# Gathering selected key and value blocks as pairs in rows of eight tokens, in a hybrid attention and convolution layer

## The chip, the cores and the metric

The kernel runs on one core of a Trainium2 chip as one program. The metric is device time in microseconds (us) of one execution; before the change it is 1492.12 us, the median of 3 runs (1490.02 to 1495.15). Engines are named as in the profile: PE is TensorE, PEld its weight loads, DVE VectorE, ACT ScalarE, POOL GpSimd, SP the engine that only issues transfers.

## The reference

One inference step of one decoder layer, for a prompt of 1024 tokens and for 8 samples of 4 new tokens each with 8192 past tokens in paged caches. One projection of the normalised input gives queries, three key/value sets, gates and the input of a convolution module. What the change touches is one of three attention branches of the samples: per query and group of heads, the 16 best of 128 blocks of 64 tokens are attended to. Three blocks (the first, the last cached one, the new one) are always among them. Cut to what matters:

```
forced = (j == 0) | (j == cur) | (j == cur - 1)
score = jnp.where(forced[None, :, None, :], FORCED_SCORE, imp)
_, idx = lax.top_k(score, n_top)                       # n_top = 16
k_sel = ks_bg[b_i, g_i, idx].reshape(B, N_KV, Q, n_sel, HEAD_DIM)
v_sel = vs_bg[b_i, g_i, idx].reshape(B, N_KV, Q, n_sel, HEAD_DIM)
s_s = jnp.einsum('bqghd,bgqnd->bqghn', qf, k_sel)
p_s = masked_softmax(s_s, m_s)
o_s = jnp.einsum('bqghn,bgqnd->bqghd', p_s.astype(v_sel.dtype), v_sel)
```

So per query and group there are 13 chosen blocks and 2 forced cached ones, besides the 4 new tokens.

## The kernel before, in words

The program has three phases that share one projection of weight tiles (`project`, lines 241 to 255: three matmuls of 352 columns for each piece, lines 183 to 185). Phase 1 (to about 565 us) normalises the input, gathers all compressed-branch pages (`load_pool`, line 503) and ends with `choose` (line 716), which ranks the blocks and writes `idxs`, a table of row numbers for the gathers. Phase 2 (about 565 to 920 us) interleaves three streams by `_weave` (line 1194): `sample_stream` (the selected blocks and the window branch), `conv_ins` (projections, named mm in the rows), and `conv_stream` (31 convolution taps on DVE, line 1157). Phase 3 is the prompt's attention and the output projections.

In phase 2 there are 8 units u. A unit is one group of heads g and two samples times four new tokens. The cached tables are seen as rows of four tokens (2 KB, line 137), so a block of 64 tokens is 16 rows, and one gather (`gather`, line 933) of 128 rows fills a tile of 128 partitions x 512 with one chosen block for each of 8 (sample, token) pairs.

- `slc_keys(u)` (line 947) loops over 7 steps of two tiles each: 13 gathers into `KG` (6 buffers, `KB`) and, as the fourteenth, a tile of forced blocks. ACT copies the group's half of each tile to `kg` (line 975), PE turns it (two transposes, line 978), ACT copies the four turned pieces to `skT` (line 982), PE multiplies with the queries (line 956), and DVE adds a mask while it writes the scores (line 959).
- `slc_vals(u)` (line 1022) runs beside the keys of unit u+1: four steps, each with four gathers into `VG` (6 buffers, `VB`; the last step has one), transposes of the scores (line 1044), a copy (line 1052), and the products of the step before (line 1034).
- `forced` (line 939) gathers the forced blocks of four samples at once into `Fk_slc` and `Fv_slc`: four gathers in all, with row numbers `idxF` made at the start of phase 1 (lines 369 to 382, with DVE's line 378).

Each engine works its instructions in order. The order is set when the program is built, by a scheduler that runs a timeline of its own. The gathers all stand in POOL's queue, KG and VG mixed; each waits there until its buffer is free, and those behind it wait too. A buffer of KG is free when ACT's copy has read it, one of VG when PE's products have.

## Time and profile before

| | |
|---|---|
| median of 3 runs | 1492.12 us |
| the profiled execution | 1496.63 us, span 1494.8 us |
| PE busy | 1370.8 us (92%) |
| DVE, ACT, POOL busy | 1094.9 us (73%), 729.5 us (49%), 786.2 us (53%) |
| mean granted TensorE clock | 0.969 of full |
| gathers KG, VG | 104 and 104, busy 123.3 and 113.5 us on POOL |
| moved by software queue q0 (all gathers) | 122.71 MB in 37440 packets |

Busy time is the time in which an engine had an instruction of its own running. The idle time before a group of instructions is named with what ended it. Matmuls are pipelined, so the durations of single ones overlap. The granted clock is a share of full speed in the stretch that the row names.

### The profile page before, as it was taken

What the parts mean: (1) busy time and instruction counts of PE and PEld (TensorE: products, weight loads), DVE (VectorE), ACT (ScalarE), POOL (GpSimd) and SP (SyncE); (2) the same over time, 40 slices, a digit from 0 to 9 for tenths busy, and PEclk for the clock granted to TensorE, in tenths of its full rate; (3) what the DMA queues carried; (4) which work ended last, traced back from release to release, by engine and by line L of the source; (5) the groups of instructions that cost most, each with busy time, mean ns of one, the idle gap of its engine ahead of it and who ended that gap; (6) DMA issues with size and microseconds to landing.
All of it is one profiled execution on the core that took longest, in us unless ns stands there. A gap on an engine that the chain in (4) does not pass through costs nothing.

```text
span 1494.8 us, 25906 instructions
## 1 busy us (share of the span) xinstructions
PE 1370.8 (92%) x9687; PEld 1214.4 (81%) x9687; DVE 1094.9 (73%) x1949; ACT 729.5 (49%) x1384; POOL 786.2 (53%) x646
## 2 busy tenths in 40 slices
PE   2998999998999998998999999999979999899997
PEld 1897889887988997776777778888968999789876
DVE  8878786878888847876765842697877888888333
ACT  4454454454443532543444433676666776663311
POOL 5487774776875618778777740244465222311200
PEclk9899999999999999999999999999989999999999
DMA  7666556575566517676778754633273543516421
GB/s 235 211 197 213 167 183 196 178 213 183 185 194 198 176 47 218 197 234 205 230 227 256 250 177 147 177 108 96 88 207 109 160 131 97 144 34 212 157 103 54
DMA packets 185191, 253.74 MB, mean 170 GB/s; under 512 B 28947, under 2 KB 139107, under 8 KB 184802
## 3 DMA queue, kind: packets, MB, share of 16 engines
q1 hardware_dynamic: 137114, 121.42, 26.8%
q0 software_dynamic: 37440, 122.71, 26.6%
q10 hardware_dynamic: 10512, 7.96, 1.7%
q8 instruction: 76, 1.25, 0.3%
q14 instruction: 49, 0.40, 0.1%
HBM read 212.42 MB, written 44.20 MB: 172 GB/s over the span
## 4 chain that ended last, share of the span: by engine, by line
PE 40%; DMA 23%; DVE 14%; issue 10%; POOL 8%; ACT 3%; SPq 1%; ACTq 0%; POOLq 0%; DVEq 0%
DMA G<-in_cache_v_cmp,idxc 6%; DMA G<-in_cache_k_cmp,idxc 6%; POOL G L503 6%; DMA VG<-in_cache_v_slc,idxs 5%; PE v L183 3%; PE v L185 3%; PE v L184 3%; PE mm L184 3%; PE mm L185 3%; PE mm L183 3%; PE tr L183 3%; PE tr L184 3%; PE tr L185 3%; DMA KG<-in_cache_k_slc,idxs 2%; PE tr L1440 2%
## 5 line engine op out<-in xcount | busy, mean ns | idle before, releaser
L183 PE MATMUL mm<-xh,wh 128*128 128x352 f32 x840 | 281.0, 335 | 0.9 <-ACT stg L262 0.4
L184 PE MATMUL mm<-xl,wh 128*128 128x352 f32 x840 | 280.1, 333 | 0.0
L185 PE MATMUL mm<-xh,wl 128*128 128x352 f32 x840 | 279.6, 333 | 0.0
L461 DVE STREAM_TRANSPOSE T<-G 128x512 f32<-128x512 f32 x260 | 175.6, 697 | 80.8 <-DMA G<-in_cache_k_cmp,idxc 37.6
L503 POOL DMA_INDIRECT G<-in_cache_v_cmp,idxc x128 | 171.0, 1336 | 83.0 <-DVE T L461 49.9
L465 ACT ACTIVATE Th<-T 128x2048 fp32r<-128x2048 f32 x66 | 124.8, 1891 | 162.2 <-DVE T L461 136.9
L503 POOL DMA_INDIRECT G<-in_cache_k_cmp,idxc x128 | 167.2, 1306 | 64.8 <-DVE T L461 26.4
L183 PEld LDWEIGHTS mm<-xh,wh 128*128 128x128 f32 x840 | 162.3, 193 | 8.4 <-issue 5.9
L185 PEld LDWEIGHTS mm<-xh,wl 128*128 128x128 f32 x840 | 162.3, 193 | 8.2 <-issue 7.2
L184 PEld LDWEIGHTS mm<-xl,wh 128*128 128x128 f32 x840 | 162.5, 193 | 6.8 <-issue 5.3
L1157 DVE SCALAR_TENSOR_TENSOR acc<-ub,dwT,acc 128x1024 f32<-128x1024 f32 x120 | 154.3, 1286 | 1.2
L469 DVE TENSOR_TENSOR Tl<-T,Th 128x2048 fp32r<-128x2048 f32 x66 | 146.8, 2225 | 3.9 <-ACT Th L465 3.8
L934 POOL DMA_INDIRECT KG<-in_cache_k_slc,idxs x104 | 123.3, 1185 | 37.9 <-issue 19.5
L934 POOL DMA_INDIRECT VG<-in_cache_v_slc,idxs x104 | 113.5, 1091 | 40.9 <-issue 15.0
L1265 DVE TENSOR_TENSOR ptl<-tr,pth 128x512 fp32r<-128x512 f32 (+1 forms) x152 | 100.2, 670 | 22.3 <-ACT pth L1264 21.4
L1415 POOL TENSOR_SCALAR P<-P,sc 128x640 f32<-128x640 f32 (+4 forms) x32 | 52.9, 1652 | 106.0 <-DVE sc L1408 63.9
L1354 ACT ACTIVATE P<-S,sc 128x640 f32<-128x640 f32 (+7 forms) x128 | 89.3, 701 | 35.7 <-PE tr L1440 18.7
L1264 ACT ACTIVATE pth<-tr 128x512 fp32r<-128x512 f32 (+1 forms) x152 | 87.6, 585 | 36.6 <-PE tr L1440 29.9
L451 PE MATMUL x<-Tl,w1hk 128*128 128x256 f32 (+1 forms) x264 | 77.3, 293 | 14.4 <-DVE Tl L469 14.1
L1440 PE MATMUL tr<-ident,P 128*128 128x128 f32 x528 | 80.5, 277 | 3.8 <-DVE gbt L1629 2.5
L1431 PE MATMUL acc<-ptl,vs 128*128 128x256 f32 x264 | 73.4, 300 | 10.2 <-DVE ptl L1265 9.8
L451 PE MATMUL x<-Tl,w1hv 128*128 128x256 f32 (+1 forms) x264 | 76.6, 290 | 6.5 <-DVE Tl L469 6.4
(468 smaller groups left out, 3672.6 us busy)
## 6 DMA issues: line engine op xcount, KB each, us to landing
wt<-in_w_in SPq DMA_DIRECT2D x42, 512.0 KB
m_d<-stg SPq DMA_DIRECT2D x16, 528.0 KB
x<-in_x_prompt SPq DMA_DIRECT2D x16, 512.0 KB
mb<-m_d SPq DMA_DIRECT2D x24, 176.0 KB
t_d<-mb SPq DMA_DIRECT2D x24, 176.0 KB
mb<-t_d SPq DMA_DIRECT2D x24, 176.0 KB
ma<-m_d SPq DMA_DIRECT2D x24, 176.0 KB
ldq<-qT_d SPq DMA_DIRECT2D x32, 128.0 KB
```

Source lines behind the costliest of these rows:

```text
L183: pe.matmul(ps, wh, xh, start=i == 0, stop=False)
L184: pe.matmul(ps, wh, xl, start=False, stop=False)
L185: pe.matmul(ps, wl, xh, start=False, stop=i == n - 1)
L451: pe.matmul(o, w[:, s], t[:, :, :, s // 2, s % 2], start=s == 0 and i == 0, stop=s == 7 and i == 2)
L461: dve.transpose(T[:, gi], G)
L465: act.activation(Th[:, :m], T[:, :m], AF.Copy)
L469: eng.tensor_tensor(Tl[:, r], T[:, r], Th.bitcast(F32)[:, r], op=ALU.subtract)
L503: pool.indirect_dma_start(out=G, out_offset=None, in_=tab, in_offset=bass.IndirectOffsetOnAxis(ap=idxc[:, b * 16 + gi:b * 16 + gi + 1], ax ...
L934: pool.indirect_dma_start(out=dst, out_offset=None, in_=pools[n], in_offset=bass.IndirectOffsetOnAxis(ap=col, axis=0))
L1157: eng.scalar_tensor_tensor(a, x, dwT[:, ct, j:j + 1], a, op0=ALU.mult, op1=ALU.add)
L1265: dve.tensor_tensor(lo[:, :w], t[:, :w], hi.bitcast(F32)[:, :w], op=ALU.subtract)
L1440: pe.transpose(t[:, (2 * x + e) * 128:(2 * x + e + 1) * 128], Ps[e * 2 + i][:, c0:c0 + 128], ident)
```

## The change

The two selected-block tables are seen as rows of eight tokens (4 KB). A gather of 128 such rows fills a tile of 128 x 1024 with two blocks for each of 8 (sample, token) pairs: 8 rows per block, 64 partitions for each of the pair. Seven pairs make a unit. The thirteenth chosen block has as its partner a forced block (`rw`'s last column: the first block, or the last cached one, by the token's number), so the four gathers of `forced` and their row numbers go. There are 3 buffers for KG (were 6 of half the size), 4 for VG (were 6), 2 of double size for `kg` (were 3). ACT's copy of a pair is one instruction of 128 x 512. Transposes, score products and value products are as many as before. The masks `ms` have two planes (were three).

```diff
-NT = 13
+NP = 7
-KB = 6
-K2 = 3
+KB = 3
+K2 = 2
-VB = 6
+VB = 4
...
-    pools = {n: I["cache_" + n][0].rearrange("n (r j) g d -> (n r) (j g d)", j=4)
-             for n in ("k_cmp", "v_cmp", "k_slc", "v_slc")}
+    pools = {n: I["cache_" + n][0].rearrange("n (r j) g d -> (n r) (j g d)", j=j)
+             for n, j in (("k_cmp", 4), ("v_cmp", 4), ("k_slc", 8), ("v_slc", 8))}
...
-        for j in range(8):
-            dve.tensor_scalar(msk[:, 4 + j:5 + j], p_hi4, float(j), None, op0=ALU.is_equal)
...
-        for j in range(8):
-            dve.scalar_tensor_tensor(idF, ptv[:, j // 2, 63 * (j % 2)], msk[:, 4 + j:5 + j], idF,
-                                     op0=ALU.mult, op1=ALU.add)
-        dve.tensor_scalar(idF, idF, 32.0, p_lo5, op0=ALU.mult, op1=ALU.add)
-        idxF = ab.tile([128, 2], I32, name="idxF")
-        dve.tensor_copy(idxF, idF)
+        p_lo3 = pbits("p_lo3", 0, 7)
...
+            dve.tensor_scalar(key[:, 2:3], r_t[:64], 1.0, None, op0=ALU.is_equal)
+            dve.tensor_tensor(key[:, 3:4], rball[:, 127:128], rball[:, 0:1], op=ALU.subtract)
+            dve.scalar_tensor_tensor(rw[:, 2 * NP - 1:], key[:, 3:4], key[:, 2:3], rball[:, 0:1], op0=ALU.mult,
+                                     op1=ALU.add)
...
-            pe.matmul(p[:, :8 * NT], sel, W.rearrange("p a b -> p (a b)"), start=True, stop=True)
+            for e in range(2):
+                pe.matmul(p[e * 64:(e + 1) * 64, :8 * NP], sel, W[:, e].rearrange("p a c -> p (a c)"), start=True,
+                          stop=True, tile_position=(0, e * 64))
...
-            fixed = forced("k_slc", a_ // 2)
...
-            for c in range(7):
+            for c in range(NP):
                 t = bank(ps_tr, "tr")
-                for e in range(2):
-                    n = 2 * c + e
-                    if n < NT:
-                        kg = kp.tile([128, 512], F32, name="KG", tag="KG", bufs=KB)
-                        gather(kg, "k_slc", idxs[:, u * NT + n:u * NT + n + 1])
-                    else:
-                        kg = fixed
-                    x = kp.tile([128, 256], F32, name="kg", tag="kg", bufs=K2)
...
+                kg = kp.tile([128, 1024], F32, name="KG", tag="KG", bufs=KB)
+                gather(kg, "k_slc", idxs[:, u * NP + c:u * NP + c + 1])
+                x = kp.tile([128, 512], F32, name="kg", tag="kg", bufs=K2)
+                with sooner(HF):
+                    act.activation(x.rearrange("p (k d) -> p k d", k=8),
+                                   kg.rearrange("p (k g d) -> p g k d", k=8, g=2)[:, g], AF.Copy)
+                for j in range(4):
+                    pe.transpose(t[:, j * 128:(j + 1) * 128], x[:, j * 128:(j + 1) * 128], ident)
...
-            VG = {NT: forced("v_slc", a_ // 2)}
+            VG = {}
...
-                for n in range(4 * c, min(4 * c + 4, NT)):
-                    VG[n] = vp.tile([128, 512], F32, name="VG", tag="VG", bufs=VB)
-                    gather(VG[n], "v_slc", idxs[:, u * NT + n:u * NT + n + 1])
+                for n in range(2 * c, 2 * c + m):
+                    VG[n] = vp.tile([128, 1024], F32, name="VG", tag="VG", bufs=VB)
+                    gather(VG[n], "v_slc", idxs[:, u * NP + n:u * NP + n + 1])
```

The scheduler builds a new order from this. Two places of POOL's queue follow. The first is the start of phase 2, where the small IOTA rows make mask tables. Before:

```order
L172 IOTA nt 128x32
L934 DMA Fk_slc<-in_cache_k_slc,idxF 128x512
L934 DMA KG<-in_cache_k_slc,idxs 128x512 x6
L934 DMA Fv_slc<-in_cache_v_slc,idxF 128x512
L934 DMA VG<-in_cache_v_slc,idxs 128x512 x6
L172 IOTA tmpi 128x128
L934 DMA KG<-in_cache_k_slc,idxs 128x512 x18
```

and of the changed kernel:

```order
L173 IOTA nt 128x32
L931 DMA KG<-in_cache_k_slc,idxs 128x1024 x3
L931 DMA VG<-in_cache_v_slc,idxs 128x1024 x4
L173 IOTA tmpi 128x64
L931 DMA KG<-in_cache_k_slc,idxs 128x1024 x10
```

Ahead of the first KG gather that reuses a buffer there were fourteen gathers, and there are seven now.

The second place is the middle of phase 2, where keys of one unit and values of the unit before alternate. Before:

```order
L934 DMA VG<-in_cache_v_slc,idxs 128x512 x4
L934 DMA KG<-in_cache_k_slc,idxs 128x512 x4
L934 DMA VG<-in_cache_v_slc,idxs 128x512 x4
L934 DMA KG<-in_cache_k_slc,idxs 128x512 x2
L934 DMA VG<-in_cache_v_slc,idxs 128x512 x2
L934 DMA KG<-in_cache_k_slc,idxs 128x512 x3
```

and of the changed kernel:

```order
L931 DMA VG<-in_cache_v_slc,idxs 128x1024 x2
L931 DMA KG<-in_cache_k_slc,idxs 128x1024 x2
L931 DMA VG<-in_cache_v_slc,idxs 128x1024 x2
L931 DMA KG<-in_cache_k_slc,idxs 128x1024
L931 DMA VG<-in_cache_v_slc,idxs 128x1024 x2
```

Between one reload of VG and the next there stood two to four KG gathers of one block; now one or two of a pair stand there.

## Rows read from the trace of the kernel before

**Rows 1.** Busy time of each engine by stretch of the span (start and end in us), from the view by windows: length; busy time and instructions of PE, PEld, DVE, ACT and POOL; granted clock; share of the DMA engines; GB/s. The three phases without the first 60 us and the last part.
```profile
60.00:565.00 505.00, 476.87 (x3375) 445.13 (x3376) 395.99 (x560) 231.91 (x305) 337.00 (x261) 0.99 0.58 179
565.00:920.00 355.00, 326.51 (x2782) 262.18 (x2781) 234.26 (x475) 150.55 (x336) 243.16 (x218) 0.95 0.71 215
920.00:1350.00 430.00, 403.43 (x2739) 369.90 (x2739) 346.12 (x614) 286.55 (x620) 160.97 (x139) 0.97 0.42 125
```

**Rows 2.** Groups of POOL's instructions from 619 to 868 us, the two largest: count, busy us, mean ns of one, idle time before them and what ended it.
```profile
L934 POOL DMA_INDIRECT VG<-in_cache_v_slc,idxs x89 | 98.2, 1103 | 28.8 <-issue 13.1 <-PE tr L978 3.8 <-PE y L1034 3.6
L934 POOL DMA_INDIRECT KG<-in_cache_k_slc,idxs x79 | 90.7, 1149 | 27.7 <-issue 14.9 <-ACT kg L975 7.3 <-DMA VG<-in_cache_v_slc,idxs 1.8
```

**Rows 3.** What PE waited for from 565 to 920 us: us in total, times, longest.
```profile
PE y L1034 <- DMA VG<-in_cache_v_slc,idxs: 20.4, 19, 4.6
PE tr L978 <- ACT kg L975: 7.8, 3, 3.9
```

**Rows 4.** PE's instructions in order of time, at its longest gaps and around 700 to 716 us: start, us, instruction, and in brackets the idle time before it and what ended it.
```profile
590.75 0.69 PE L978 MATMUL tr<-ident,kg 128*128 128x128 f32 x2 [3.91 <-ACT kg L975]
...
639.01 0.69 PE L978 MATMUL tr<-ident,kg 128*128 128x128 f32 x2 [3.53 <-ACT kg L975]
...
697.91 0.56 PE L1034 MATMUL y<-VG,spT 128*32 128x64 f32 x12 [4.63 <-DMA VG<-in_cache_v_slc,idxs]
...
700.97 0.64 PE L1034 MATMUL y<-VG,spT 128*32 128x64 f32 x12 [0.67 <-DMA VG<-in_cache_v_slc,idxs]
...
703.18 0.49 PE L183 MATMUL mm<-xh,wh 128*128 128x352 f32 x1
703.47 0.49 PE L184 MATMUL mm<-xl,wh 128*128 128x352 f32 x1
...
705.08 0.32 PE L184 MATMUL mm<-xl,wh 128*128 128x352 f32 x1
705.24 0.33 PE L185 MATMUL mm<-xh,wl 128*128 128x352 f32 x1
...
713.13 0.31 PE L1034 MATMUL y<-VG,spT 128*32 128x64 f32 x4
715.70 0.64 PE L1034 MATMUL y<-VG,spT 128*32 128x64 f32 x12 [2.27 <-DMA VG<-in_cache_v_slc,idxs]
...
899.14 0.30 PE L1034 MATMUL y<-VG,spT 128*32 128x64 f32 x4 [2.31 <-DMA VG<-in_cache_v_slc,idxs]
```

**Rows 5.** Five stretches of 5 us with a lowered granted clock, by windows (columns as in Rows 1).
```profile
590.00:595.00 5.00, 4.13 (x15) 3.76 (x16) 4.93 (x8) 1.60 (x4) 4.00 (x4) 0.50 0.67 196
640.00:645.00 5.00, 5.00 (x23) 4.78 (x24) 2.94 (x7) 2.49 (x4) 4.09 (x4) 0.66 0.81 261
700.00:705.00 5.00, 4.33 (x28) 3.92 (x29) 0.00 (x0) 0.76 (x3) 4.12 (x5) 0.51 0.59 172
715.00:720.00 5.00, 4.30 (x25) 4.06 (x26) 1.56 (x2) 0.00 (x0) 4.08 (x5) 0.51 0.78 218
865.00:870.00 5.00, 5.00 (x34) 3.80 (x27) 2.94 (x5) 0.60 (x1) 3.85 (x4) 0.66 0.72 195
```

**Rows 6.** POOL's instructions in order of time at the start of phase 2 and at 632 us (columns as in Rows 4).
```profile
563.66 1.02 POOL L934 DMA_INDIRECT Fk_slc<-in_cache_k_slc,idxF  x1 [0.16 <-POOL nt L172]
...
586.70 1.00 POOL L934 DMA_INDIRECT KG<-in_cache_k_slc,idxs  x1 [0.16 <-DMA VG<-in_cache_v_slc,idxs]
...
632.86 0.95 POOL L934 DMA_INDIRECT KG<-in_cache_k_slc,idxs  x1 [0.30 <-issue]
```

**Rows 7.** The view of one tile, for KG and for VG: shortest, median and longest duration of a gather on POOL in ns, and the time from its start to its landing.
```profile
L934 POOL DMA_INDIRECT KG<-in_cache_k_slc,idxs x104: 942/1014/3866, 565.0 to 853.2; - x104
DMA to landing us min/median/max: 3.5/4.3/8.6
...
L934 POOL DMA_INDIRECT VG<-in_cache_v_slc,idxs x104: 942/950/1992, 578.9 to 894.9; - x104
DMA to landing us min/median/max: 3.2/4.0/7.9
```

**Rows 8.** The whole of phase 2's gathers and of ACT's copies, by shape, from 565 to 925 us (columns as in Rows 2).
```profile
L934 POOL DMA_INDIRECT KG<-in_cache_k_slc,idxs x104 | 123.3, 1185 | 37.9 <-issue 19.5 <-ACT kg L975 11.2 <-DMA VG<-in_cache_v_slc,idxs 2.0
L934 POOL DMA_INDIRECT VG<-in_cache_v_slc,idxs x104 | 113.5, 1091 | 40.9 <-issue 15.0 <-PE y L1034 10.8 <-PE tr L978 3.8
L975 ACT ACTIVATE kg<-KG 128x256 f32<-128x256 f32 x104 | 42.7, 413 | 79.2 <-DMA KG<-in_cache_k_slc,idxs 42.6 <-PE tr L978 20.3 <-issue 14.6
L982 ACT ACTIVATE skT<-tr 128x512 f32<-128x512 f32 x56 | 33.0, 589 | 16.3 <-PE tr L978 15.7
```

**Rows 9.** Two stretches of 5 us with the DMA engines full, and the stretch in which `choose` runs, by windows (columns as in Rows 1).
```profile
565.00:570.00 5.00, 5.00 (x34) 4.90 (x33) 4.97 (x27) 0.80 (x3) 4.39 (x3) 1.00 1.04 333
800.00:805.00 5.00, 5.00 (x51) 4.35 (x50) 2.44 (x8) 3.21 (x5) 3.78 (x5) 1.00 1.04 357
...
480.00:500.00 20.00, 19.81 (x147) 19.36 (x145) 16.54 (x45) 12.55 (x17) 6.82 (x5) 1.00 0.41 120
```

**Rows 10.** The start of phase 1 in order of time on DVE and POOL (columns as in Rows 4): the row numbers of the forced blocks, the first scaled input, the multiplication before it.
```profile
8.69 2.25 DVE L378 SCALAR_TENSOR_TENSOR idF<-ptb,msk,idF 128x2 f32<-128x2 f32 x1
...
12.15 0.81 DVE L354 TENSOR_SCALAR x<-x,ss 128x1024 f32<-128x1024 f32 x1
...
8.42 2.50 POOL L348 TENSOR_TENSOR x<-x,gB 128x1024 f32<-128x1024 f32 x1 [6.82 <-DMA gB<-in_ln_g]
```

More of the change, by code (lines that the diff above doesn't have):

```diff
@@ L310, in _emit @@
         dve.tensor_scalar(offc, p_c8, 4.0, p_a, op0=ALU.mult, op1=ALU.add)
-        msk = ca.tile([128, 12], F32, name="msk")
+        msk = ca.tile([128, 4], F32, name="msk")
         for j in range(4):
@@ L712, in prompt_cmp @@
             yield
-        idxs = ab.tile([128, 8 * NT], I32, name="idxs")
+        idxs = ab.tile([128, 8 * NP], I32, name="idxs")
         def choose():
@@ L751, in choose @@
             rb = TA[:64, 384:].rearrange("p (a b) -> p a b", b=2)
-            dve.tensor_scalar(rb[:, :, 0], pr64, 32.0, None, op0=ALU.mult)
-            dve.tensor_scalar(rb[:, :, 1], rb[:, :, 0], 16.0, None, op0=ALU.add)
-            rbv = rb.rearrange("p a b -> p (a b)")[:, 1:127]
+            dve.tensor_scalar(rb[:, :, 0], pr64, 16.0, None, op0=ALU.mult)
+            dve.tensor_scalar(rb[:, :, 1], rb[:, :, 0], 8.0, None, op0=ALU.add)
+            rball = rb.rearrange("p a b -> p (a b)")
+            rbv = rball[:, 1:127]
             io = TA[:, 256:384]
             iota_f(io, [[1, 128]])
-            rw = cpl.tile([64, NT], F32, name="rw", tag="rw", bufs=1)
-            for n in range(NT):
-                oh = TB[:64, :126]
-                dve.scalar_tensor_tensor(oh, io[:64, :126], mf[:, n:n + 1], rbv, op0=ALU.is_equal,
-                                         op1=ALU.mult, accum_out=rw[:, n:n + 1])
             r_t = pbits("r_t", 0, 3)
@@ L765, in choose @@
             r_bp = pbits("r_bp", 4, 3)
-            key = cpl.tile([64, 2], F32, name="key", tag="key", bufs=1)
+            rw = cpl.tile([64, 2 * NP], F32, name="rw", tag="rw", bufs=1)
+            for n in range(2 * NP - 1):
+                oh = TB[:64, :126]
+                dve.scalar_tensor_tensor(oh, io[:64, :126], mf[:, n:n + 1], rbv, op0=ALU.is_equal,
+                                         op1=ALU.mult, accum_out=rw[:, n:n + 1])
+            key = cpl.tile([64, 4], F32, name="key", tag="key", bufs=1)
+            dve.tensor_scalar(key[:, 2:3], r_t[:64], 1.0, None, op0=ALU.is_equal)
+            dve.tensor_tensor(key[:, 3:4], rball[:, 127:128], rball[:, 0:1], op=ALU.subtract)
+            dve.scalar_tensor_tensor(rw[:, 2 * NP - 1:], key[:, 3:4], key[:, 2:3], rball[:, 0:1], op0=ALU.mult,
+                                     op1=ALU.add)
             dve.scalar_tensor_tensor(key[:, 0:1], r_b2[:64], 4.0, r_t[:64], op0=ALU.mult, op1=ALU.add)
             dve.scalar_tensor_tensor(key[:, 1:2], r_bp[:64], 2.0, r_g[:64], op0=ALU.mult, op1=ALU.add)
-            io8 = TC[:64, :128].rearrange("p (a b) -> p a b", b=16)
-            iota_f(io8, [[1, 8], [0, 16]])
-            sel = TB[:64, 128:256]
+            io8 = TC[:64, :64].rearrange("p (a b) -> p a b", b=8)
+            iota_f(io8, [[1, 8], [0, 8]])
+            sel = TB[:64, 128:192]
             dve.tensor_scalar(sel, io8.rearrange("p a b -> p (a b)"), key[:, 0:1], None, op0=ALU.is_equal)
@@ L774, in choose @@
             dve.tensor_scalar(wm, io[:64, :8], key[:, 1:2], None, op0=ALU.is_equal)
-            W = TB[:64, 256:256 + 8 * NT].rearrange("p (a b) -> p a b", b=NT)
-            dve.tensor_tensor(W, rw[:, None, :].to_broadcast([64, 8, NT]),
-                              wm[:, :, None].to_broadcast([64, 8, NT]), op=ALU.mult)
-            p = bank(ps_tr, "tr")
-            pe.matmul(p[:, :8 * NT], sel, W.rearrange("p a b -> p (a b)"), start=True, stop=True)
-            isf = TB[:, 384:384 + 8 * NT]
-            dve.tensor_scalar(isf, p[:, :8 * NT], p_lo4, None, op0=ALU.add)
+            W = TB[:64, 256:256 + 16 * NP].rearrange("p (e a c) -> p e a c", e=2, c=NP)
+            rwv = rw.rearrange("p (c e) -> p e c", e=2)
+            for e in range(2):
+                dve.tensor_tensor(W[:, e], rwv[:, e, None, :].to_broadcast([64, 8, NP]),
+                                  wm[:, :, None].to_broadcast([64, 8, NP]), op=ALU.mult)
+            p = bank(ps_tr, "tr")
+            for e in range(2):
+                pe.matmul(p[e * 64:(e + 1) * 64, :8 * NP], sel, W[:, e].rearrange("p a c -> p (a c)"), start=True,
+                          stop=True, tile_position=(0, e * 64))
+            isf = TB[:, 384:384 + 8 * NP]
+            dve.tensor_scalar(isf, p[:, :8 * NP], p_lo3, None, op0=ALU.add)
             dve.tensor_copy(idxs, isf)
@@ L935, in gather @@
                                     in_offset=bass.IndirectOffsetOnAxis(ap=col, axis=0))
-        FX = {}
-        def forced(n, q4):
-            if (n, q4) not in FX:
-                FX[n, q4] = bc.tile([128, 512], F32, name="F" + n, tag="F" + n)
-                gather(FX[n, q4], n, idxF[:, q4:q4 + 1])
-            return FX[n, q4]
         S_ = {}
```

36 lines of the change are left out of this document (10 added, 26 removed).

## The prediction

> **What bounds the kernel now.** I read the busy times by stretch first. PE is the bound nearly everywhere: busy 477 of 505 us in phase 1, 403 of 430 in phase 3. Phase 2 is the loosest: 326.5 of 355 us, at a granted clock of 0.95 [rows 1]. The change works in phase 2, so that stretch decides.
>
> What lets PE wait there? Its list of waits has two lines: 20.4 us for VG gathers (19 times) and 7.8 us for ACT's copy of a KG tile (3 times) [rows 3]. Together 28.2 us, and 355 - 326.5 gives the same 28.5. The clock comes on top. After the gaps of 3.9, 3.5 and 4.6 us at 590, 639 and 698 us [rows 4] the granted clock falls to its lower level for a few us: 0.50, 0.66 and 0.51 in the stretches that follow [rows 5]. Matmuls then start 0.29 us apart, and 0.16 once it is back [rows 4]: that is 1.2 GHz and 2.4 GHz. Over the phase the loss is (1 - 0.95) x 326.5 = 16.3 us. So the phase holds **28.5 + 16.3 = 44.8 us** that PE's own work doesn't need. This is the ceiling of what any change of the gathers can give here.
>
> Why are gathers late? POOL, which issues them, is never free. From 619 to 868 us its 168 gathers of VG and KG are busy 98.2 + 90.7 us and have 28.8 + 27.7 us before them: 245.4 of 249 us [rows 2]. About 0.30 us stands before each gather that waits for nothing [rows 6], so one costs 1.14 + 0.30 = 1.44 us (1.14: 123.3 + 113.5 us over 208 [rows 8]). The KG that ends the gap at 639 was issued at 632.86 [rows 6], behind values; the first reload of KG stands at 586.70, 23 us after the phase's first gather at 563.66 [rows 6], and the gap at 590.75 waits for it. POOL's queue paces PE.
>
> **The change part by part, against the profiled execution of 1496.6 us.**
>
> *Fewer gathers.* 212 (208 and four forced ones) become 8 x 14 = 112. A gather of a pair has 128 rows as now, each twice as long. No row shows one of 4 KB rows. By the number of rows it takes 1.14 us, by the bytes 2.28; the shortest, 0.94 us, is alike in both tiles [rows 7] and all have 128 rows. I take 1.14: the count of rows stays, only their length changes. POOL's issue then falls from 212 x 1.44 = 305 us to 112 x 1.44 = 161 us, half of the phase. POOL is on the path only through late gathers, so what this gives is read from PE's gaps.
>
> *The start of the phase.* The first reload of KG stands behind 7 gathers in place of 14. 563.7 + 7 x 1.44 = 573.8, against 586.7. It lands well before 590: the 3.9 us and the low clock behind them go.
>
> *Keys.* Three pairs of buffers hold the same six blocks as before. A reload takes about 1.4 us of issue and the landing, 4.3 us now [rows 7]. A pair has 0.26 MB more, 0.8 us at the 333 GB/s of a full stretch [rows 9]; the ends are 4.3 (nothing more) and 8.6 (the longest seen [rows 7]); I take 5.1. The gap at 639 came from POOL's backlog and goes. Of the 7.8 us about 0.4 stay.
>
> *Values.* Here the buffers grow: four pairs hold two whole steps, six blocks held one and a half. Before, the last two gathers of a step waited for the products just ahead of them; after, a step's gathers wait for products two steps back. In the trace two steps are 700.97 to 713.13, 12.2 us [rows 4]; at full clock about 10. A reload of two pairs needs 0.3 + 1.14 + 0.3 for the second to start, up to two KG gathers between (2 x 1.44), and the landing, 4.0 + 0.8: 6.5 to 9.4 us. That just fits. With single blocks, one step of 5 to 6 us stood against 0.3 + 1.1 + 0.3 + 4.0 = 5.7 us and up to four KG gathers more, 11.5: the gaps of 2.3 to 4.6 us. I leave 1 us for each of 8 units, 8 us, and the 2.3 us of the last one at 899 [rows 4], where only values are left. Bounds: 2.3 us (all fits) and 20.4 (nothing gained).
>
> *What is left of 44.8:* gaps 0.4 + 8 + 2.3 + 0.3 (unnamed) = 11 us. Of six spells of low clock (five in [rows 5], a short one behind 899), 16.3 / 6 = 2.7 us each, I keep two: 5.5 us. The gain is 44.8 - 16.5 = 28.3 us.
>
> *More bytes.* Forced blocks are now fetched for every unit: 112 x 0.524 against 212 x 0.262 MB, 3.1 MB more, 9 us of full DMA. The DMA share is 0.71 at 215 GB/s [rows 1]; with this and a phase 27 us shorter it is 0.80. Hidden on the mean; I take 1 us (0 to 3).
>
> *ACT.* 112 copies at 0.413 us become 56 of twice the size, between 0.589 (the skT copy of that shape) and 0.83 us [rows 8]: 0 to 13 us less on an engine that is busy 151 of 355 us [rows 1]. Nothing, since PE waits for it only through the gather. If the copy came late, 0.2 us per pair would be the price.
>
> *Small work.* At the start DVE loses its row numbers of forced blocks, one of which took 2.25 us beside POOL's multiplication. That multiplication ends at 10.9 and the first scaled input starts at 12.15 [rows 10]: 0 to 1.2 us, I take 0.5. In `choose` three small operations and a matmul are added where PE is busy 19.8 of 20 us with other work [rows 9]: nothing; uncovered, under 1 us. The masks are built while PE is full (5.00 of 5.00 [rows 9]): nothing. The rest of the order moves slightly, worth plus or minus 2 us, as the runs differ (1490 to 1495).
>
> **Sum:** 28.3 - 1 + 0.5 = 27.8, in round numbers 27 us since a spell more or less is 2.7: 1469.6 for the profiled execution, which was 4.5 us above the median. Against the median: 1492.1 - 27 = **1465 us**, within 1450 (2.3 us of gaps and one spell of low clock left) and 1475. A measurement here tells 0.3% (4.5 us) from no change.
>
> **The rivals.**
>
> *Bursts fill the DMA engines (0.15).* From 697.91 to 715.70 PE takes three groups of values [rows 4], now six pairs, and as POOL's order runs up to five of keys: 11 x 0.524 = 5.8 MB in 17.8 us, 324 GB/s, beside weight tiles, where full is 333 to 357 [rows 9]. For it: that. Against: seven pairs are fetched ahead. Then all 20.4 us of the values' waits stay with their low clock; what goes is the keys' 7.8 us and two of the six spells, 5.4 us. With the 0.5 us of the start that is 14 us, **1478 us**.
>
> *A gather costs by its bytes (0.08).* Then it doesn't do what it says: 112 x (2.28 + 0.30) = 289 us of issue against 305. POOL stays full; the gain is 0 to 8 us, **1488 us**. Against: no duration in rows 7 hangs on bytes, but all have the same number.
>
> *Landing takes the place of issue (0.09), the other side.* If two pairs land later than the two steps cover (a landing over 10 - 1.7 = 8.3 us, where 8.6 is the longest seen [rows 7]), PE waits at the same 22 places, each 0.8 us longer, and nothing is recovered: 22 x 0.8 = 18 us, **1510 us**. POOL's order makes it possible: a VG gather that waits for PE keeps KG gathers behind it. Against: medians of 4.0 and 4.3 us, and a POOL that has half its time free. The Trainium skill speaks for this rival (page "DMA: Bandwidth & Descriptors", section "Anatomy of one DMA — SWDGE (gpsimd) path"): generating descriptors is small, and about 2 us of completion plus the bytes over 436 GB/s are the cost. By that page a gather is 2.6 us and a pair 3.2, and POOL's issue would not be a limit, so halving the count would give nothing and cost 0.6 us per landing. The rows differ: 0.94 us at the least on POOL for each gather, and POOL full for 249 us, which is why this rival gets no more.
>
> **How the numbers follow.** The forecast has 0.68. Faster by over 0.3% (under 1487.6): 0.68 + 0.15 + 0.02 of the bytes' case = 0.85. Within: 0.06 of that case. Slower: 0.09. The range reaches down to 1449, nearly the whole ceiling recovered, and up to 1487, which takes in the burst case and leaves the other two out: about 8 in 10.
>
> **What would show it.** Right: 112 gathers at about 1.1 us; POOL busy near 130 of some 330 us and idle between gathers for buffers; landings near 5 us; PE's waits for VG and kg near 11 us; one to three spells of low clock; phase 2 about 27 us shorter, the other phases within 2 us. Wrong: gathers above 2 us; DMA share near 1 in most of the phase; PE's waits above 20 us, or moved to kg; a phase 3 that is longer because its start waits for the changed phase's buffers.

## The result, and the profile after

The changed kernel takes **1450.27 us** (median of 4 runs, 1448.92 to 1452.58), the kernel before 1492.97 beside it (4 runs, 1490.02 to 1495.15): a ratio of **0.9717, 95% interval 0.9693 to 0.974**. The forecast was 1465 us, a gain of 27; the gain is 42.7. The kernel is faster in the stretch that was named, and its trace shows the reason that was named, but I had left 16.5 us of the loss in place, of which little stayed. The time lies at the low end of what I gave, which is partly luck (see below).

The three phases of the changed kernel, by windows (columns as in rows 1; phase 2 ends about 40 us earlier, so the bounds are moved):

```profile
60.00:565.00 505.00, 477.17 (x3377) 446.21 (x3377) 394.19 (x558) 232.96 (x305) 336.53 (x257) 0.99 0.58 177
565.00:880.00 315.00, 309.79 (x2834) 258.22 (x2834) 237.85 (x485) 147.63 (x287) 138.58 (x124) 0.99 0.78 261
880.00:1310.00 430.00, 401.43 (x2718) 368.04 (x2717) 347.99 (x610) 283.39 (x615) 159.26 (x137) 0.97 0.42 122
```

Against [rows 1]: phases 1 and 3 are nearly as they were. In phase 2 PE idles 5 of 315 us where it idled 28.5 of 355, the granted clock is 0.99 for 0.95, and POOL is busy 44% of the time for 68%.

To compare the same work, take the stretch from the first gather of phase 2 to the first score matmul of phase 3 (S at L1305 before, L1287 after): PE runs 2947 instructions in it in both kernels. First the kernel before, then the one after:

```profile
563.70:945.00 381.30, 352.81 (x2947) 288.48 (x2946) 243.72 (x491) 161.10 (x354) 245.87 (x221) 0.96 0.72 215
```

```profile
565.70:898.50 332.80, 327.59 (x2947) 276.04 (x2946) 241.72 (x487) 154.04 (x298) 138.03 (x121) 0.99 0.77 257
```

The stretch is 48.5 us shorter. PE's idle time fell by 23.3 (28.5 to 5.2), its busy time by 25.2. The clock accounts for about 11 of these (0.04 x 352.8 against 0.01 x 327.6, two-digit clocks). Part of the rest is in the value products, 896 in both kernels. Before, they were busy 33.66 us (832 of VG and 64 of the forced tile, line 1034 alone in the stretch; the two kinds overlap):

```profile
563.70:945.00 381.30, 33.66 (x896) 19.77 (x896) 0.96 0.72 215
```

and now

```profile
L1016 PE MATMUL y<-VG,spT 128*32 128x64 f32 x896 | 22.8, 224 | 1.9 <-DMA VG<-in_cache_v_slc,idxs 1.9
```

The mean of one is nearly the same (230 and 224 ns); they overlap more, 25 ns of busy time for each in place of 38. The clock's part and the products' overlap, since the products too ran partly at the lower clock. Before the stretch the changed kernel is 2.0 us later, behind it 2.5 us slower (552.3 for 549.8 us to the end), so that the profiled executions differ by 44.0 (1496.6 and 1452.6).

What PE waits for from 565 to 880 us (compare [rows 3]: 20.4 us in 19 waits and 7.8 in 3):

```profile
PE tr L1026 <- ACT Ss L982: 3.3, 1, 3.3
PE y L1016 <- DMA VG<-in_cache_v_slc,idxs: 1.9, 3, 0.9
```

The keys no longer appear, the values nearly not. POOL's two groups in that stretch, against [rows 2, 8]:

```profile
L931 POOL DMA_INDIRECT VG<-in_cache_v_slc,idxs x56 | 68.8, 1228 | 50.2 <-PE y L1016 36.6 <-issue 8.1 <-PE y L1047 2.5
L931 POOL DMA_INDIRECT KG<-in_cache_k_slc,idxs x56 | 63.6, 1135 | 80.1 <-ACT kg L958 60.7 <-issue 6.1 <-DMA KG<-in_cache_k_slc,idxs 4.8
```

A gather takes 1.18 us on the mean, where it took 1.14. What changed is the idle time ahead of it: 130 us, of which 97 for a buffer still in use (PE's products, ACT's copy). POOL now runs ahead and waits for its consumers; before, they waited for it. The landings, by the view of one tile (KG, then VG), against [rows 7]:

```profile
L931 POOL DMA_INDIRECT KG<-in_cache_k_slc,idxs x56: 935/996/1887, 565.7 to 800.9; - x56
DMA to landing us min/median/max: 4.3/7.5/9.4
...
L931 POOL DMA_INDIRECT VG<-in_cache_v_slc,idxs x56: 935/1150/1913, 569.8 to 834.9; - x56
DMA to landing us min/median/max: 4.5/6.2/9.1
```

By the medians a pair lands 2.2 to 3.2 us later than a single block did, and PE hardly waits for it. Two stretches of 5 us with full DMA engines, and the only one of this phase whose clock is down (the columns of rows 1):

```profile
570.00:575.00 5.00, 5.00 (x34) 4.98 (x33) 5.00 (x14) 0.63 (x1) 4.39 (x3) 1.00 1.02 389
755.00:760.00 5.00, 5.00 (x51) 4.31 (x51) 1.30 (x9) 3.31 (x7) 1.65 (x2) 1.00 1.04 404
...
795.00:800.00 5.00, 3.72 (x18) 3.72 (x19) 4.89 (x11) 4.30 (x10) 0.94 (x1) 0.66 0.22 60
```

These two show 389 and 404 GB/s where [rows 9] showed 333 and 357, but stretches of 5 us with full engines (a share of 1.00 or more) differ: 353 to 420 GB/s from 570 to 870 us here, 314 to 357 from 565 to 920 us in the kernel before. The gathers have a DMA queue of their own, q0: packets, MB, and the time of its packets as a share of all engines' time. Before (560 to 900 us), then after (560 to 840 us):

```profile
q0 software_dynamic: 16919, 55.48, 54.7%
...
q0 software_dynamic: 16122, 58.71, 59.9%
```

While its packets move, that is 298 GB/s before (55.48 MB in 0.547 x 340 us) and 350 now. Longer packets are not the reason: in the trace the data of a gather move in packets of 4096 bytes in both kernels, 64 for a gather of single blocks (so two rows of 2 KB in one) and 128 for a pair. Their median time is the same, 159 ns; the mean fell from 217 to 186 ns (600 to 860 us before, 600 to 830 us after). The one spell of low clock stands behind the one long gap, and that has another cause: DVE waited for the buffer of the convolution's sums, and through it ACT and PE (DVE, then PE, in order of time):

```profile
791.75 0.81 DVE L1141 TENSOR_SCALAR acc<-ub,dwT,vT 128x1024 f32<-128x1024 f32 x1 [7.48 <-DMA c_d<-acc]
...
796.28 1.11 PE L1026 MATMUL tr<-ident,Ss 128*128 128x128 f32 x4 [3.34 <-ACT Ss L982]
```

### The profile page after: what moved, and what is told of

It is laid out like the page before. It is cut to its first block, busy times and chain, and to the rows that moved or that the text cites. A ratio compares the mean times of both kernels' runs of the same rounds, so it can differ in the third digit from the quotient of the medians.

```text
span 1450.8 us, 25622 instructions
## 1 busy us (share of the span) xinstructions
PE 1347.5 (93%) x9689; PEld 1204.6 (83%) x9689; DVE 1095.5 (76%) x1926; ACT 722.5 (50%) x1328; POOL 679.2 (47%) x546
## 4 chain that ended last, share of the span: by engine, by line
PE 51%; DMA 20%; DVE 13%; issue 7%; POOL 6%; ACT 2%; SPq 1%; DVEq 0%; POOLq 0%; ACTq 0%
DMA G<-in_cache_v_cmp,idxc 7%; DMA G<-in_cache_k_cmp,idxc 6%; POOL G L491 5%; PE mm L184 5%; PE mm L186 5%; PE mm L185 5%; PE v L184 3%; PE v L186 3%; PE v L185 3%; PE tr L184 3%; PE tr L186 3%; PE tr L185 3%; DVE T L449 3%; PE tr L1422 2%; DVE Tl L457 2%
## 5 line engine op out<-in xcount | busy, mean ns | idle before, releaser
L184 PE MATMUL mm<-xh,wh 128*128 128x352 f32 x840 | 277.9, 331 | 0.9 <-ACT stg L263 0.4
L186 PE MATMUL mm<-xh,wl 128*128 128x352 f32 x840 | 275.3, 328 | 0.0
L185 PE MATMUL mm<-xl,wh 128*128 128x352 f32 x840 | 274.6, 327 | 0.0
L1336 ACT ACTIVATE P<-S,sc 128x640 f32<-128x640 f32 (+7 forms) x128 | 89.2, 701 | 37.3 <-PE tr L1422 19.6
L931 POOL DMA_INDIRECT KG<-in_cache_k_slc,idxs x56 | 63.6, 1135 | 80.1 <-ACT kg L958 60.7
L931 POOL DMA_INDIRECT VG<-in_cache_v_slc,idxs x56 | 68.8, 1228 | 50.2 <-PE y L1016 36.6
```

The lines of the kernel that those rows point to most:

```text
L184: pe.matmul(ps, wh, xh, start=i == 0, stop=False)
L185: pe.matmul(ps, wh, xl, start=False, stop=False)
L186: pe.matmul(ps, wl, xh, start=False, stop=i == n - 1)
L931: pool.indirect_dma_start(out=dst, out_offset=None, in_=pools[n], in_offset=bass.IndirectOffsetOnAxis(ap=col, axis=0))
```

## The experiments

Theories. **A, issue:** every gather holds POOL for a nearly fixed time; 212 of them filled its queue, 112 leave it room. **B, depth:** the gain is that of the value buffers, which hold eight blocks in place of six. **C, rows:** the gain is that of longer rows, whose transfers move faster. **D, copy:** one ACT copy of 128x512 in place of two of 128x256. The runs came in three groups, each on another chip, and the kernel before doesn't take the same time on all: 1533.35 us in the first (e2 to e5), 1491.66 in the second (r_before to e6), 1532.07 in the third (r_after2, e9, e10, e5_again). The changed kernel does where it ran: 1450.27 us at first (on a chip that isn't known, beside the kernel before at 1492.97), 1450.99 in the second group and 1449.93 in the third. In the first group only variants of it ran, of which e2 and e5 took 1453 and 1444. So I compare changed kernels with each other, in us; where I give a ratio, it is to the kernel before on the same chip.

**e2_vb3: six blocks of value buffers, as before.**

```
-VB = 4
+VB = 3
```

> The changed kernel with 3 buffers of pairs for VG in place of 4, so six blocks as before the change. Theory A (issue: the gain comes from half as many gathers in POOL's queue): the gain stays, 1450 to 1456 us, PE's waits for VG under 6 us. Rival B (depth: the gain comes from VG's buffers, which grew from six to eight blocks): most of the gain goes, 1475 to 1490 us, PE's waits for VG back near 20 us.

Measured: 1453.17 us (1452.09 to 1454.53), ratio 0.9476 (0.944 to 0.9512). What PE waits for from 565 to 900 us:

```profile
PE y L1016 <- DMA VG<-in_cache_v_slc,idxs: 6.5, 6, 2.7
```

The waits grow from 1.9 to 6.5 us, the time by 2 to 3 against the changed kernel on other chips. B falls as the main cause: with the old depth nearly all the gain is there.

**e3_more: a second gather behind each, with rows of 64 bytes.**

The edit, without the line that views the table in rows of 64 bytes (`short`):

```
+            d = vp.tile([128, 16], F32, name="DG", tag="DG", bufs=8)
+            pool.indirect_dma_start(out=d, out_offset=None, in_=short,
+                                    in_offset=bass.IndirectOffsetOnAxis(ap=col, axis=0))
```

> The changed kernel with a second gather of 128 rows of 64 bytes behind each gather of a pair, into a tile that nothing reads: 224 gathers in POOL's queue as there were 212 before, the data and the buffers of the changed kernel. Theory A (issue): POOL is full again, 224 x 1.4 = 314 us of issue, and the time is back at 1478 to 1495 us. Rival B (depth) and rival C (long rows: transfers of 4 KB rows move faster): 1450 to 1456 us.

Measured: 1554.07 us, ratio 1.0134 (1.0092 to 1.0176): all the gain gone, 104 us above the changed kernel's 1450, and far above A's 1478 to 1495. Two windows of its worst part:

```profile
600.00:620.00 20.00, 12.21 (x49) 9.29 (x49) 5.94 (x7) 3.04 (x6) 15.73 (x15) 0.76 0.44 130
620.00:640.00 20.00, 12.28 (x61) 9.13 (x61) 11.07 (x13) 5.13 (x9) 12.30 (x11) 0.63 0.32 87
```

In the first POOL's 15 instructions are busy 15.73 us, and with 0.30 us ahead of each they fill the 20; DMA's share is 0.44, PE idles 7.8 us, and the clock falls. So a full POOL queue goes with a waiting PE where the DMA engines have room. But the size says less than I meant: nothing reads these tiles, and they were issued in runs (15 of the 18 gathers from 602 to 625 us), so that real gathers stood behind them. That a queue of 224 gathers in good order would lose less is likely, and no run shows it. A gather of 64-byte rows holds POOL for 0.94 us at the least, as long as one of 4 KB rows.

**e4_halves: each pair as two gathers of 64 rows.**

The edit, without the lines that copy the row numbers of partitions 64 to 127 into `idx2`:

```
+            for r, t in ((slice(0, 64), idxs), (slice(64, 128), idx2)):
+                pool.indirect_dma_start(out=dst[r], out_offset=None, in_=pools[n],
+                                        in_offset=bass.IndirectOffsetOnAxis(ap=t[:64, col:col + 1], axis=0))
```

> The changed kernel with each pair gathered as two gathers of 64 rows of 4 KB, one for each half of the partitions: 224 gathers, the same rows, bytes, buffers and order of values. If a gather's cost on POOL is fixed (0.94 us and 0.3 before it), POOL is full and theory A says 1478 to 1495 us. If the cost goes by the rows (about 0.5 us and 0.3 before it), issue is 224 x 0.8 = 180 us and theory A says 1450 to 1458 us. Rivals B and C: 1450 to 1456 us whatever POOL does.

Measured: 1547.85 us, ratio 1.0114 (1.0064 to 1.0164), again above A's 1478 to 1495. The gathers of the keys' first and second half, by the view of one tile:

```profile
L934 POOL DMA_INDIRECT KG<-in_cache_k_slc,idxs x56: 887/896/1887, 564.7 to 893.0; - x56
L934 POOL DMA_INDIRECT KG<-in_cache_k_slc,idx x56: 892/952/1930, 566.0 to 894.3; - x56
```

64 rows take 0.89 us at the least, 128 rows 0.94, with rows of 64 bytes (e3), 2 KB [rows 7] or 4 KB alike: the price is nearly that of a gather, not of its rows or bytes. The loss looked like A's at first. It is not clean, though: the DMA engines were nearly full too, at little speed.

```profile
600.00:620.00 20.00, 19.61 (x127) 16.15 (x126) 18.61 (x27) 10.12 (x18) 12.86 (x12) 1.00 1.02 234
860.00:880.00 20.00, 15.32 (x109) 11.45 (x107) 11.68 (x21) 6.36 (x12) 13.50 (x13) 0.85 1.05 234
```

**e7_vhalves: only the value pairs in halves** (168 gathers; `gather` is that of e4, and the keys have `gather1`, one gather of 128 rows). One line of the edit:

```
-                    gather(VG[n], "v_slc", idxs[:, u * NP + n:u * NP + n + 1])
+                    gather(VG[n], "v_slc", u * NP + n)
```

> The changed kernel with each pair of value blocks as two gathers of 64 rows, the keys as pairs: 168 gathers for 112, the same bytes. Theory A (a gather occupies POOL for a nearly fixed time, and POOL's queue is the bound only once it is full): 168 x 1.3 to 1.5 us = 218 to 252 us of POOL in a stretch of about 333 us, so most of the gain stays: 1455 to 1485 us, with the loss in the parts where the value gathers follow each other. Rival P (each gather costs its own time on the path, full queue or not): half of the way back to 224 gathers, whose two kernels took 1548 and 1554: about 1500. Rival V (only the gathers of the values counted): nearly all the way back, 1530 or more.

Measured: 1499.96 us (10 runs, 1489.13 to 1510.68), ratio 1.0057 (1.0019 to 1.0095); 49 us above the changed kernel on the same chip (1450.99). That is P's number, and dearer than A's. POOL's groups from 565 to 920 us:

```profile
L934 POOL DMA_INDIRECT VG<-in_cache_v_slc,idxs x56 | 63.7, 1138 | 54.3 <-PE y L1023 39.9 <-issue 9.6 <-PE tr L968 1.8
L938 POOL DMA_INDIRECT KG<-in_cache_k_slc,idxs x56 | 63.3, 1130 | 65.5 <-ACT kg L965 44.1 <-issue 6.7 <-ACT stg L263 5.1
L934 POOL DMA_INDIRECT VG<-in_cache_v_slc,idx x56 | 60.3, 1077 | 18.6 <-issue 15.9 <-DMA KG<-in_cache_k_slc,idxs 2.4 <-DMA VG<-in_cache_v_slc,idxs 0.3
```

POOL waits 84 us for buffers, so it is not the bound and neither A nor P explains this kernel. The DMA view from 800 to 840 us does (share in tenths and GB/s, in slices of 1 us), with PE's two longest waits of phase 2, SP's issue of the store `c_d`, and the longest wait of DVE:

```profile
DMA  9999999999999999999999999999999999951000
GB/s 234 332 397 404 379 370 310 189 190 198 250 232 256 242 288 409 416 220 248 265 268 248 264 246 228 258 239 218 237 227 250 229 326 409 388 208 56 2 0 0
```

```profile
PE mm L184 <- DVE stg L265: 19.6, 1, 19.6
PE y L1023 <- DMA VG<-in_cache_v_slc,idx: 16.9, 9, 4.4
...
828.33 0.33 SPq L1156 DMA_DIRECT2D c_d<-acc  x1
...
837.10 0.81 DVE L1148 TENSOR_SCALAR acc<-ub,dwT,vT 128x1024 f32<-128x1024 f32 x1 [27.91 <-DMA c_d<-acc]
```

The engines are full for 36 us, yet for most of that at 190 to 265 GB/s, with spells of about 400. What the kernel changes is that its value gathers write 64 partitions each. Small packets of other traffic are not the reason: of the 4383 packets in these 40 us 717 are under 512 bytes, and from 750 to 790 us the changed kernel has 755 such among 5809 and moves 346 GB/s on the mean. The gathers' own queue tells the kernels apart, e4 first and e7 second, 560 to 900 us:

```profile
q0 software_dynamic: 16334, 53.57, 65.5%
...
q0 software_dynamic: 16934, 58.46, 65.4%
```

That is 241 GB/s while its packets move in e4, where all gathers write 64 partitions, 263 in e7, where half of the bytes do, and 350 in the changed kernel. With the engines full the values are late, and so is a store of SP whose buffer DVE needs, which stopped PE for 19.6 us: DVE waited from 809 us, SP issued the store only at 828.33, since its queue had stood behind other transfers since 802.70, and it landed at 837. The Trainium skill has a rule for this (page "SBUF — State Buffer", section "Door 1: The DMA port swizzle"): partitions 0 to 63 lie behind 8 of the 16 ports through which DMA reaches the memory, 64 to 127 behind the other 8, so that a transfer to 64 partitions gets half of the speed, some 218 GB/s. The trace agrees in size: 190 to 265 for 400, and 241 for 350. So e4 and e7 don't tell A from C. They show that the shape of a gather's destination can cost as much as this change gives.

**r_before and r_after: both kernels, unchanged, on one chip.**

> The kernel before, unchanged, on the chip on which it and the kernels below are timed against each other; for its trace. In an earlier group of runs the same kernel took 1533 us where it took 1493 us beside the changed kernel. If its time hangs on the chip and the issue of the gathers makes the difference (theory A), the gathers here take longer on POOL than 1.14 us each, POOL is full from the first value gather to the last, and the second stretch (381 us in the first trace) alone is longer; phases one and three stay within 3 us. If instead the whole chip is slower or its clock lower, all three phases are longer in proportion.

> The changed kernel, unchanged, on the same chip. Theory A: 112 gathers leave POOL's queue with room whatever the chip, so 1450 us again, within 3, even where the kernel before takes 1530. If the chip as a whole differs: slower in the same proportion as the kernel before.

Measured: r_before 1497.32 us in its one run, and 1491.66 in the 13 runs beside (1485.27 to 1507.66); r_after 1450.99 (1448.47 to 1452.5), ratio 0.9713 (0.9645 to 0.978). This chip gave the kernel before the shorter of its two times, so r_before says nothing of the 40 us. The stretch of the same work, before and after:

```profile
562.60:942.10 379.50, 351.76 (x2939) 287.31 (x2938) 242.53 (x487) 161.14 (x354) 247.03 (x220) 0.96 0.72 214
```

```profile
563.90:897.70 333.80, 327.77 (x2946) 275.17 (x2946) 241.55 (x487) 154.25 (x298) 136.25 (x121) 0.99 0.76 256
```

Both readings of the first traces (381.3 and 332.8 us) come again within 2 us.

**e9_fill and e10_half: POOL's queue made longer, the transfers left alone.**

```
         def gather(dst, n, col):
+            pool.memset(dst, 0.0)
```

That is e9; e10 fills `dst[:, :512]`, half of the tile.

> The changed kernel with a memset of the whole 128x1024 tile on POOL ahead of each of the 112 gathers: no DMA, packet or byte more, only POOL's queue is longer. From the rows of POOL's fills (128x256 in 0.27 to 0.30 us) 128x1024 takes about 1.1 us, so 112 x (1.14 + 0.30 + 1.2) = 296 us of POOL, nearly the 305 us of the kernel before. Theory A (POOL's queue was the bound): most of the gain goes, 1478 to 1500 us, with POOL full between the value gathers and PE waiting for VG and kg again. Rival C (the gain is that of the long rows on the DMA engines, which were nearly full with short ones; the two kernels with 64-row gathers lost it because their transfers ran at 240 to 290 GB/s at a full share): 1450 to 1458 us, since the transfers are the same.

> The same with a memset of half the tile (128x512, about 0.6 us): 112 x 2.04 = 228 us of POOL in a stretch of about 333. Theory A with a knee (POOL costs nothing while its queue has room): 1450 to 1460 us. A without a knee (each 1 us of POOL costs its share at once): half the loss of the full memset, 1465 to 1475. Rival C: 1450 to 1455.

> The changed kernel, unchanged, beside the three others of this group: 1448 to 1454 us.

Measured, on one chip: r_after2 1449.93 us (6 runs, 1448.06 to 1456.17), e10_half 1456.83 (4 runs, 1449.52 to 1471.6), e9_fill 1465.32 (4 runs, 1463.41 to 1473.44). The stretch of the same work in r_after2, e10_half and e9_fill:

```profile
562.90:897.70 334.80, 327.91 (x2947) 275.22 (x2946) 241.20 (x487) 152.96 (x298) 137.10 (x121) 1.00 0.76 255
```

```profile
561.40:899.20 337.80, 330.11 (x2947) 276.00 (x2946) 246.03 (x488) 152.78 (x298) 194.30 (x234) 0.99 0.77 251
```

```profile
563.50:909.90 346.40, 331.11 (x2947) 277.64 (x2946) 256.57 (x488) 153.38 (x298) 242.77 (x233) 0.99 0.76 245
```

e9 is 15 us slower, its runs clear of r_after2's, with nearly the same DMA share and clock. It is outside both forecasts, C's 1450 to 1458 and A's 1478 to 1500; POOL's need came out smaller than I had taken. POOL's groups of e9 from 565 to 900 us, and PE's wait for the values from 565 to 920:

```profile
L932 POOL DMA_INDIRECT VG<-in_cache_v_slc,idxs x56 | 66.8, 1194 | 12.3 <-issue 7.0 <-POOL KG L931 2.6 <-POOL VG L931 2.0
L932 POOL DMA_INDIRECT KG<-in_cache_k_slc,idxs x56 | 66.8, 1192 | 14.2 <-issue 8.5 <-POOL KG L931 3.9 <-POOL VG L931 1.1
L931 POOL MEMSET KG<- 128x1024 f32 x55 | 52.8, 966 | 14.4 <-ACT kg L959 14.0 <-issue 0.4
L931 POOL MEMSET VG<- 128x1024 f32 x56 | 52.7, 964 | 12.5 <-PE y L1017 11.8 <-PE x L945 0.7
```

```profile
PE y L1017 <- DMA VG<-in_cache_v_slc,idxs: 6.1, 6, 2.3
```

In the three traces of the changed kernel PE waited 1.9, 2.4 and 0.6 us for the values, with the same transfers: the 4 to 5 us more go with the longer queue. That C is the whole cause doesn't fit this.

But the fills do something that I hadn't expected. DVE's busy time grows with them over the same instructions, 241.20, 246.03 and 256.57 us in the three rows above. At the start of phase 2 in e9 it can be seen, DVE first, then POOL:

```profile
562.65 7.13 DVE L868 COPY gw<-gcw 32x2 f32<-32x2 f32 x4
...
563.45 2.73 POOL L931 MEMSET KG<- 128x1024 f32 x3
566.14 3.62 POOL L931 MEMSET VG<- 128x1024 f32 x4
```

The last of these four copies took 6.39 us, from 563.39 to 569.78, and ended with POOL's seven fills (569.76); in e10 the longest took 3.41, without fills (r_after2) 0.30. So DVE's copy stood while POOL filled. PE waited 3.5 us behind these copies and 2.4 us for DVE's `stg` (565 to 920 us); r_after2 has neither. About half of PE's added waiting in e9 therefore comes through DVE and not through late gathers.

What POOL needs here is 66.8 + 66.8 + 112 x 0.965 + 26.5 = 268 us, not 296: no 0.30 us stands ahead of a fill. With the other kernels counted alike, need against stretch:

| kernel | POOL's need for the gathers | stretch of the same work |
|---|---|---|
| r_after2 | 112 x (1.18 + 0.30) = 166 us | 334.8 us |
| e10_half | 132 + 112 x 0.53 + 27 = 218 | 337.8 |
| e9_fill | 268 | 346.4 |
| before, r_before | 212 x 1.44 = 305 | 381.3, 379.5 |

For e9 the stretch holds 11.6 of the 16.8 us between its traced run and r_after2's; the other 5 lie outside it and are not explained.

The first 52 us cost 3 (three traces of the changed kernel spread over 2), the next 50 cost 9, of which some are DVE's, the last 37 come with 33 to 35. That looks like A with a knee, where POOL's need comes up to the 270 us over which the gathers are wanted (565.7 to 834.9 in the changed kernel), but the table doesn't prove it: the doses of e9 and e10 are not of the queue alone. The last step is not an experiment on its own: the kernel before differs in more than its queue, and the slower transfers may have a part in these 33 to 35 us. e10's runs scatter by 22 us; without the highest (1471.6) the other three have 1449.52 to 1459.0, so that its loss is not sure; its traced run was the fastest of the four.

**e5_copies and e5_again: two ACT copies per key pair, on two chips.**

```
-                    act.activation(x.rearrange("p (k d) -> p k d", k=8),
-                                   kg.rearrange("p (k g d) -> p g k d", k=8, g=2)[:, g], AF.Copy)
+                    for h in range(2):
+                        act.activation(x.rearrange("p (k d) -> p k d", k=8)[:, h * 4:(h + 1) * 4],
+                                       kg.rearrange("p (k g d) -> p g k d", k=8, g=2)[:, g, h * 4:(h + 1) * 4],
+                                       AF.Copy)
```

> The changed kernel with ACT's copy of each pair split into two of 128 x 256, as before the change: 56 instructions and some 11 us more on ACT. Theories A, B and C: nothing, 1448 to 1454 us. Rival D (the merged copy is part of the gain, since the transposes wait for it): 1456 to 1465 us.

> The changed kernel with two copies of ACT per key pair in place of one of 128x512, beside the changed kernel on the same chip. On another chip it took 1444.5, where the changed kernel has taken 1450.3 and 1451.0 on two chips. If the two smaller copies let PE's transposes start on the first half sooner: 1443 to 1447 again, 3 to 7 us below the changed kernel. If that was the chip: within 2 us of it.

Measured: 1444.47 us (1440.88 to 1447.86) on the one, 1447.97 (6 runs, 1444.44 to 1450.92) on the other beside r_after2's 1449.93. D falls: the merged copy gives nothing. Whether two copies are better by 2 us is less than these runs can tell; the 6 us of the first group were not a fair comparison, without the changed kernel on it.

**e6_acc2: a second buffer for the sums that DVE waited for, paid with one value pair.**

```
-VB = 4
+VB = 3
-            acc = cv.tile([128, TT], F32, name="acc", tag="acc", bufs=1)
+            acc = cv.tile([128, TT], F32, name="acc", tag="acc", bufs=2)
```

> The changed kernel with three buffers for the value pairs in place of four, and in the room that this frees a second buffer for the sums of the smaller convolution, for which DVE waited 7.5 us at 784 us of the changed kernel's trace (its copy out of the buffer had not landed), which held ACT, then PE for 3.3 us, behind which one window ran at 0.66 of the clock. With three buffers alone the kernel took 1453.2. Theory: the wait, the gap and the window go: 4 to 6 us less, 1447 to 1450. Rival (DVE has work enough behind it, or the wait moves to the next buffer): 1452 to 1455, no change against three buffers alone.

Measured: 1467.45 us (1464.91 to 1472.83), ratio 0.9826 (0.9754 to 0.9899): 16 us slower than r_after on the same chip, outside both forecasts. DVE's wait for `c_d` is gone, but two windows, e6 first and r_after second, show what came for it:

```profile
620.00:640.00 20.00, 14.99 (x179) 9.39 (x177) 18.57 (x41) 12.70 (x24) 14.57 (x14) 0.83 0.94 344
640.00:660.00 20.00, 10.81 (x144) 6.60 (x140) 18.14 (x40) 8.62 (x17) 14.94 (x14) 0.74 0.95 331
```

```profile
620.00:640.00 20.00, 18.17 (x154) 13.82 (x151) 12.71 (x38) 10.47 (x22) 10.39 (x11) 0.91 0.95 349
640.00:660.00 20.00, 20.00 (x207) 15.21 (x205) 17.71 (x29) 10.26 (x20) 14.11 (x12) 1.00 0.84 285
```

DVE is nearly full in both windows and PE loses 12.4 us against r_after's, most of the 16 with the clock on top. The longest of PE's waits in e6's two windows are for values, 4.8 us, then for ACT's `Ss`, 3.7; from 565 to 920 us PE waited 11.7 us for them, where r_after waited 2.4 and e2, with three buffers too, 6.5. So the lost buffer has a large part in it. That DVE took up the convolution earlier, ahead of the score sums that PE needs, may be the rest; it is not shown, since no run took the two edits apart. So no version beats the changed kernel clear of the noise here.

## Why the prediction came out as it did

- **That the ranges hold the number is partly luck.** I gave two, 1450 to 1475 in the sum and 1449 to 1487 behind the chances, and 1450.27 us lies 0.3 and 1.3 us inside their low ends. Those ends don't follow from my terms: with what I named for 1450, 2.3 us of gaps and one spell of 2.7, the gain is 44.8 - 5.0 - 1 + 0.5 = 39.3 us, which makes 1452.8. The gain was 1.6 times the 27 us.
- **The bound and the place** were right as far as the traces show: PE's waits for late gathers stood in phase 2, where POOL's queue was full. After the change POOL waits for buffers, and PE's waits for KG and VG are 1.9 us for 28.2. The experiments bear it out in part: e3 has a full queue and a waiting PE while DMA has room, and e9 has 4 to 5 us more of waiting for values with a longer queue and the same transfers. None takes the queue's share of the 43 us apart from that of the transfers.
- **The price of a gather** was right (1.14 taken, 1.18 measured), its reason only half so. I reasoned that the count of rows stays. e4 shows that half of the rows cost 0.89 for 0.94, e3 that rows of 64 bytes cost 0.94 too: neither rows nor bytes matter much. Here the Trainium skill's page "DMA: Bandwidth & Descriptors" (section "Anatomy of one DMA — SWDGE (gpsimd) path") calls the generating of descriptors small and most of a DMA's fixed time completion. The rows differ: each gather holds POOL for about a microsecond, and that decides this kernel.
- **The step that failed is the residual:** "I leave 1 us for each of 8 units, 8 us, and the 2.3 us of the last one", and two spells of low clock, 5.5 us. Of these 10.3 us of value waits 1.9 are left, and one spell in place of two, behind a gap that the gathers don't cause. I had set a reload of 6.5 to 9.4 us against 10 us and said that it just fits. The landing was even longer than I took (medians of 6.2 us for VG and 7.5 for KG, for 4.8 and 5.1), so the reload's own time was not set too high. The mistake was to charge a wait at each unit for a bound that just fits: POOL, with half of its time free, issues as soon as a buffer comes free, and the buffers hold two steps. Even with six blocks (e2) the waits are only 6.5 us.
- **The ceiling of 44.8 us was too low.** It counted idle time and clock, and took PE's busy time at full clock as fixed. The stretch gave 48.5: the value products alone were busy 10.9 us less (33.66 and 22.8). That their busy time had waits in it that the view of waits doesn't name is what I take from e4, whose tiles are late again in the changed order and whose 896 products have 32.9 us:

```profile
L1019 PE MATMUL y<-VG,spT 128*32 128x64 f32 x896 | 32.9, 234 | 15.7 <-issue 14.6 <-DMA VG<-in_cache_v_slc,idx 1.1
```

  So late tiles and a lower clock can bring it back without the old order; in e7, where few but long waits stand, they have 25.0, so lateness alone doesn't set it. The order may have a part too: in PE's order of time the products stood in 73 unbroken runs before, in 45 after and in 49 in e4, and fewer runs overlap more. No run takes these apart.
- **The start of the phase:** right. The first reload of KG was forecast for 573.8 us and came at 577.6 (the first gather itself was 2.0 us later); the gap at 590 us and its spell are gone.
- **The keys:** 0.4 us forecast, none measured.
- **More bytes:** a DMA share of 0.80 forecast, 0.77 measured, and no wait of phase 2 from it. The 1 us charged for them, less the 0.5 us for DVE at the start, stand against 4.5 us that phases 1 and 3 lost together. DVE's first scaled input did come 1.1 us earlier (11.06 us for 12.15), but the first gather started 2.0 us later. No run tells what these 4.5 us are.
- **The rivals.** The bursts did fill the engines, in stretches that moved 353 to 420 GB/s where I had taken 333 to 357, and PE's waits for the values stayed at 1.9 us. A price by bytes is refuted by the mean of 1.18 us. Landing did take longer, up to 9.4 us, beyond the 8.3 from which I had it decide, and yet PE hardly waited: that point held for a gather issued at the last moment, and they no longer were.
- **Depth** was my reason for the values' gain. e2 prices it at 3 us, so it is not the larger part (in e6's order the lost buffer cost more).

**Open:** why the kernel before takes 1532 us in two groups of runs and 1492 in the other two, while the changed one takes 1450 in the three in which it ran. The groups differ by chip, but also by time, and the chip of the first result isn't known. The kernel before was traced only where it gave the shorter time. Its granted clock over the span was 0.962 to 0.971 in the runs of the third group and 0.968 to 0.981 in those of the second, so PE rests more there, but what it waits for is not known. On the chip of the third group the gain is 82 us, and POOL's need by itself, whose price there was at most 15 us up to 268 us, doesn't account for all of it unless the last 37 us cost 67. Open too is how much of the 43 us the faster transfers have (298 and 350 GB/s), and why they are faster, with packets of the same size.

## What to carry to other kernels

Count the gathers and multiply by their time on the issuing engine, its gaps included, before looking at bytes: where that product comes near the stretch in which they are wanted (305 us for a phase of 355 here), the queue is the first suspect, and half as many gathers of twice the length gave 43 us. When a queue gets half of its time back, don't charge a small wait at each place where it used to be late: it issues ahead, and the later landings did no harm here. When you lengthen a queue to test it, see what the added work does to the other engines: fills on POOL held DVE. And keep a gather's destination 128 partitions wide: two halves of 64 cost more here than the pairing gained.
